# The dt projection moved into the first slot with its softplus steps issued without a break, the input squares moved later, and the SSD input projections of groups 1 to 7 in the two-instruction form

## The chip, the cores and the metric

The kernel runs on one core of a Trainium2 chip. The metric is device time in microseconds (us) of one launch; the profile also gives the span from the first to the last instruction of one profiled execution. Engines are named as in the profile: PE (matrix multiply) and PEld (its weight loads), DVE (vector), ACT (scalar, activations and copies), POOL and SP (which here only starts transfers). Each engine takes its instructions in the order in which they stand in its queue.

## The reference, cut to what matters

One layer with a sequence of 256 positions and width 2048: a Mamba-2 SSD mixer, a cross-attention and a gated FFN with a convolution, each as x + RMSNorm(f(RMSNorm(x))). The change touches the SSD mixer's input side:

```python
h = _rmsnorm(x, norm_pre[i, 0])
proj = h @ w_in                       # z 4096, x|B|C 6144, dt 64 columns
z, xbc, dt = jnp.split(proj, [SSD_D_INNER, SSD_D_INNER + SSD_CONV_DIM], axis=-1)
xbc = jax.nn.silu(_causal_dwconv(xbc, conv_w, conv_b))
dt = jax.nn.softplus(dt + dt_bias)
a = dt * (-jnp.exp(a_log))
a_cs = jnp.cumsum(a, axis=-1)
decay = jnp.exp(jnp.where(causal, a_cs[..., :, None] - a_cs[..., None, :], -jnp.inf))
y_diag = jnp.einsum('bgjcls,bcsgjp->bclgjp', cb[:, :, None] * decay, xdt)
```

Eight groups share B and C; each group has 8 of the 64 heads, that is four blocks of 128 columns of x and four of z.

## The kernel before

All matrices are fp32. To multiply them to fp32 accuracy on PE, each operand is split into a rounded part `hi` and a rest `lo` (`fp32r`), and three products are summed. A weight chunk of 128 columns by 2048 rows (1 MB) is loaded by SP into one of three `raw` buffers, and split in two halves of 8 row blocks: ACT copies `hi`, DVE subtracts `lo`. There are five buffers for `hi` halves and five for `lo` halves, so ACT may write a new half when PE has finished with the half five before it.

The input x lies transposed in `m` (16 row blocks of 128 by 256 positions). It is scaled by the norm's gain and split into `H[:, k]`, whose first 256 columns are `hi` and whose last 256 are `lo`. The norm's factor per position (`x_norm.rbc`, tile `rx`) comes later, since it commutes with the projection: `x_scaled` multiplies it in when a block's sum is taken out of PSUM. For the factor, ACT squares pairs of row blocks (`x_sq`), DVE adds the squares into `xacc`, eight tiny matmul records sum over partitions (`pe1`), POOL takes the power, and PE spreads it (`pe2`).

The projections run slot by slot. A slot has one or more lanes; a lane is one chunk, 16 row blocks k of three matmuls each (`mm3`: whi by x's hi, whi by x's lo, wlo by x's hi, 256 columns each), summed in one of four PSUM banks `pj`. The order of chunks is C0 and B0 together in slot 0, dt in a slot of its own, then x0, z0, x1, z1, x2, z2, x3, z3 of group 0, then C1, B1, x4, z4 and so on. The output projection's two halves stand after B4 and at the end. They, and the FFN, use `mm2`: whi by the 512 columns of x's hi and lo side by side, and wlo by x's hi in the upper half of the bank; the two halves of the bank are added when it is taken out. Work beside the matmuls is hooked to a slot and a place in it, and a scheduler with its own timeline decides each engine's final order from there, with `hot` for high priority.

The dt chunk has 64 columns, so its `hi` and `lo` are packed as one 128-column weight (`split_hi`, `split_lo` with kind "dt"), with two matmuls per k (`dt_mm`). `dt2` then turns its sum by a tiny matmul with `fold`, and computes the softplus in some 20 small DVE steps on 128 x 128 and one Exp on ACT; `dt3` sums along positions, `dt4` transposes the result and stores it to DRAM, from where `load_rows` reads it back spread over the partitions, and `decay`, `decay_exp` and `mk_m` make the masked decay matrices that `y_mm` needs.

Of the kernel before, what the change touches and what calls it, by code (L numbers as in the profile page):

```python
# [54 lines left out]

class Slot:
# [5 lines left out]
def hybrid_layer_kernel(ctx, tc, xT, memT, pvd, alog, w_dt, w_in, w_kv, w_q, w_out, w_o, w_up, w_dn, out):  # L62
    nc = tc.nc
    V, S, P, PE = nc.vector, nc.scalar, nc.gpsimd, nc.tensor
# [27 lines left out]
    B = {}  # L92
# [36 lines left out]
    def split_hi(c, h):  # L129
        kind = chunks[c][2]  # L130
        if kind == "dt":
            if h == 0:
                hi = splitp.tile([128, 1024], FR, name="hi")
                lo = splitp.tile([128, 1024], FR, name="lo")
                hi_t[c, 0], lo_t[c, 0] = hi, lo
                r = raw_t[c][:, :1024].rearrange("p (k n) -> p k n", n=64)
                for t, q in ((hi, 0), (lo, 8)):
                    S.activation(t.rearrange("p (k a n) -> p k a n", a=2, n=64)[:, :, 0], r[:, q:q + 8], AF.Copy)
            return
        a, b = span(c, h)  # L140
        hi_t[c, h] = g_part(c, h, 0) if c in in_g else splitp.tile([128, 1024], FR, name="hi")
        with behind(B.get("hold_s") if c in held else None):
            S.activation(hi_t[c, h][:, :b - a], raw_t[c][:, a:b], AF.Copy)  # L143

    def split_lo(c, h):
        kind = chunks[c][2]
        if kind == "dt":
            if h == 0:
                r = raw_t[c][:, :1024].rearrange("p (k n) -> p k n", n=64)
                for t, q in ((hi_t[c, 0], 0), (lo_t[c, 0], 8)):  # L150
                    t4 = t.rearrange("p (k a n) -> p k a n", a=2, n=64)
                    V.tensor_tensor(t4[:, :, 1], r[:, q:q + 8], t4[:, :, 0].bitcast(F32), op=OP.subtract)
            return
# [209 lines left out]
    def x_sq(j):  # L363
        sq = wA.tile([128, 2, T], F32, name="rows" if j else "xacc", bufs=4 if j else 1)
        S.activation(sq, pair(j), AF.Square)
        x_norm.add(sq)

    def x_scaled(ps, name="ev"):

        t = wA.tile([128, T], F32, name=name, bufs=2 if name == "ev" else 1)  # L370
        V.tensor_tensor(t, ps[:, :T], x_norm.rbc, op=OP.mult)  # L371
        return t

    def x_h(j):
        def fn():
            for k in range(2 * j, 2 * j + 2):
                now(hilo(halves(H[:, k]), m[:, k], col("pre", k)))
# [24 lines left out]
    def dt2():  # L402
# [22 lines left out]
        yield  # L425
# [3 lines left out]
        for t in range(2):  # L429
            V.scalar_tensor_tensor(a[:, t * NH:(t + 1) * NH], dtt[:, t], -1.0, nega, op0=OP.mult, op1=OP.mult)  # L430
# [194 lines left out]
    for kind, i in order:  # L625
        pos[kind, i] = 0 if kind == "B" and i == 0 else slot()
# [6 lines left out]
    for kind, i in order:  # L633
        s = pos[kind, i]
        if kind in ("C", "B"):
            blk = 32 + (8 if kind == "C" else 0) + i
            lane(s, w_in[blk_no], 2048, movH, bc_post(kind + "T", blk))
            blk_no += 1
            if kind == "B":
                hook(s + 2 if i else s + 3, "pe", cb_mm(i), 2 if i else 14)  # L640
        elif kind == "dt":
            c_dt = new_chunk(w_dt, 1024, "dt")
            slots[s].lanes.append((c_dt, 0, movH, hot(dt_post), dt_mm(c_dt), False))
            hook(s + 1, "pe", hot(dt2), 2)
            hook(s + 2, "pe", hot(dt3), 4)
            hook(s + 2, "pe", hot(dt4), 11)
        elif kind == "x":
            lane(s, w_in[blk_no], 2048, movH, xs_post(i))
            blk_no += 1
            d = 2 if i < 2 else 0  # L650
            if i == 0:
                for q in range(4):
                    hook(s + 2, "early", hot(load_rows(q)))
                    hook(s + 3, "early", decay(q))
                hook(s + 3, "early", decay_exp)
# [23 lines left out]
        elif kind == "z":  # L679
            lane(s, w_in[blk_no], 2048, movH, z_post(i))  # L680
# [391 lines left out]

    for j in range(KD // 2):
        if j % 2 == 0:
            hook(0, "pe", lambda j=j: w_first(j // 2), 4 * j)
        hook(0, "pe", x_h(j), 4 * j)
# [5 lines left out]
    for i, s in enumerate(slots):  # L1082
# [3 lines left out]
        if i == 0:  # L1086
            state["limit"] = 4
# [21 lines left out]
        names = ("pj", "pj", "pt", "py") if i == first_up else ("pj",) * 4  # L1109
# [138 lines left out]
```

## Time and profile before

| | |
|---|---|
| median of 3 runs | 1559.62 us (1558.85 to 1560.28) |
| the profiled execution's own time | 1559.15 us |
| its span | 1557.3 us |
| PE busy | 1541.5 us (99%) |
| DVE busy | 1199.2 us (77%) |
| ACT busy | 963.9 us (62%) |

The SSD input projections fill the stretch from 28.42 us to about 600 us, with the output projection's first half in between; group 1 is the stretch from 76.10 to 139.60 us, group 5 that from 418.10 to 480.60 us, and the FFN fills the stretch from 900 to 1400 us. PE is nearly always busy, so what counts is how many columns and instructions PE has to take, and where it has to wait for the others. A matmul's busy time in the profile overlaps the next one's; its pace is read from starts.

### The profile page before, as it was taken

What the parts mean: (1) busy time and instruction counts of PE and PEld (TensorE: products, weight loads), DVE (VectorE), ACT (ScalarE), POOL (GpSimd) and SP (SyncE); (2) the same over time, 40 slices, a digit from 0 to 9 for tenths busy, and PEclk for the clock granted to TensorE, in tenths of its full rate; (3) what the DMA queues carried; (4) which work ended last, traced back from release to release, by engine and by line L of the source; (5) the groups of instructions that cost most, each with busy time, mean ns of one, the idle gap of its engine ahead of it and who ended that gap; (6) DMA issues with size and microseconds to landing.
All of it is one profiled execution on the core that took longest, in us unless ns stands there. A gap on an engine that the chain in (4) does not pass through costs nothing. (4 is left out here: it accounts for less than half of the span.)

```text
span 1557.3 us, 26009 instructions
## 1 busy us (share of the span) xinstructions
PE 1541.5 (99%) x10364; PEld 1418.0 (91%) x10364; DVE 1199.2 (77%) x1903; ACT 963.9 (62%) x1566; POOL 11.3 (1%) x16
## 2 busy tenths in 40 slices
PE   9999999999999999999989999999999999999998
PEld 8999999989999999889888888888888888888886
DVE  7699989755898987969788878655787866778774
ACT  7698887644777774856566655544555533555553
POOL 0000000000000000000000000000000000000000
PEclk9999999999999999999999999999999999999999
DMA  7665555655455554854444555555555555555452
GB/s 278 212 217 189 174 203 190 194 191 184 162 204 177 167 186 136 324 189 165 161 153 146 194 190 189 192 183 199 190 191 191 184 187 198 194 192 189 151 212 78
DMA packets 50937, 292.10 MB, mean 188 GB/s; under 512 B 5568, under 2 KB 9728, under 8 KB 23936
## 3 DMA queue, kind: packets, MB, share of 16 engines
q1 hardware_dynamic: 50096, 289.34, 54.3%
q8 instruction: 81, 1.33, 0.3%
q10 hardware_dynamic: 720, 1.11, 0.2%
q14 instruction: 40, 0.33, 0.1%
HBM read 288.26 MB, written 2.16 MB: 186 GB/s over the span
## 5 line engine op out<-in xcount | busy, mean ns | idle before, releaser
L143 ACT ACTIVATE hi<-raw 128x1024 fp32r<-128x1024 f32 (+2 forms) x518 | 539.9, 1045 | 480.9 <-PE pj L252 378.4
L157 DVE TENSOR_TENSOR lo<-raw,hi 128x1024 fp32r<-128x1024 f32 (+2 forms) x518 | 624.4, 1207 | 252.7 <-ACT hi L143 247.9
L252 PE MATMUL pj<-H,hi 128*128 128x512 f32 x1344 | 466.6, 392 | 1.1 <-DVE ev L931 1.1
L252 PE MATMUL pj<-G,hi 128*128 128x512 f32 x1202 | 417.1, 392 | 0.0
L246 PE MATMUL pj<-H,hi 128*128 128x256 f32 x1344 | 379.1, 283 | 1.3 <-ACT hi L266 0.8
L248 PE MATMUL pj<-H,lo 128*128 128x256 f32 x1344 | 377.9, 282 | 0.8 <-DVE lo L268 0.7
L247 PE MATMUL pj<-H,hi 128*128 128x256 f32 x1344 | 377.8, 281 | 0.0
L253 PE MATMUL pj<-H,lo 128*128 128x256 f32 x1344 | 376.2, 280 | 0.0
L253 PE MATMUL pj<-G,lo 128*128 128x256 f32 x1202 | 335.8, 280 | 0.0
L252 PEld LDWEIGHTS pj<-H,hi 128*128 128x128 f32 x1344 | 252.3, 188 | 57.0 <-ACT hi L143 1.3
L252 PEld LDWEIGHTS pj<-G,hi 128*128 128x128 f32 x1202 | 225.4, 188 | 49.5
L246 PEld LDWEIGHTS pj<-H,hi 128*128 128x128 f32 x1344 | 253.3, 189 | 3.2 <-ACT hi L266 1.6
L248 PEld LDWEIGHTS pj<-H,lo 128*128 128x128 f32 x1344 | 253.3, 189 | 2.1 <-DVE lo L268 1.7
L247 PEld LDWEIGHTS pj<-H,hi 128*128 128x128 f32 x1344 | 253.7, 189 | 1.2 <-DVE H L272 0.2
L253 PEld LDWEIGHTS pj<-H,lo 128*128 128x128 f32 x1344 | 252.5, 188 | 0.1
L253 PEld LDWEIGHTS pj<-G,lo 128*128 128x128 f32 x1202 | 225.8, 188 | 0.4
L941 DVE SCALAR_TENSOR_TENSOR fu<-ev,pv,fu 128x255 f32<-128x255 f32 (+1 forms) x176 | 84.3, 480 | 2.8
L460 DVE SCALAR_TENSOR_TENSOR u<-ev,pv,u 128x255 f32<-128x255 f32 (+2 forms) x144 | 68.7, 479 | 5.1 <-ACT u L456 3.9
L937 ACT ACTIVATE fu<-ev,pv 128x256 f32<-128x256 f32 x88 | 51.7, 589 | 1.4 <-DVE ev L934 0.9
L371 DVE TENSOR_TENSOR ev<-pj,rx 128x256 f32<-128x256 f32 x80 | 33.7, 422 | 13.4 <-PE pj L248 10.7
L266 ACT ACTIVATE Mh<-dec 128x768 fp32r<-128x768 f32 x32 | 26.9, 841 | 16.4 <-PE py L248 15.6
L934 DVE TENSOR_TENSOR ev<-ev,rb 128x256 f32<-128x256 f32 x84 | 35.5, 422 | 1.4
(287 smaller groups left out, 1461.7 us busy)
## 6 DMA issues: line engine op xcount, KB each, us to landing
raw<-in_w_up_dram SPq DMA_DIRECT2D x88, 1024.0 KB, 4.8
raw<-in_w_in_dram SPq DMA_DIRECT2D x78, 1024.0 KB, 4.9
raw<-in_w_out_dram SPq DMA_DIRECT2D x32, 1024.0 KB, 4.8
raw<-in_w_dn_dram SPq DMA_DIRECT2D x32, 960.0 KB, 4.7
raw<-in_w_dn_dram SPq DMA_DIRECT2D x16, 896.0 KB, 4.4
rows<-rows_d SPq DMA_DIRECT2D x32, 256.0 KB, 4.4
raw<-in_w_kv_dram SPq DMA_DIRECT2D x4, 1024.0 KB, 4.8
raw<-in_w_kv_dram SPq DMA_DIRECT2D x8, 512.0 KB, 4.3
```

Of the source, the lines that this page charges most:

```text
L143: S.activation(hi_t[c, h][:, :b - a], raw_t[c][:, a:b], AF.Copy)
L157: V.tensor_tensor(lo_t[c, h][:, :b - a], raw_t[c][:, a:b], hi_t[c, h][:, :b - a].bitcast(F32), op=OP.subtract)
L246: PE.matmul(ps, whi, xhi, start=start, stop=False)
L247: PE.matmul(ps, whi, xlo, start=False, stop=False)
L248: B["mm"] = PE.matmul(ps, wlo, xhi, start=False, stop=stop)
L252: PE.matmul(ps, whi, x, start=start, stop=False)
L253: B["mm"] = PE.matmul(ps[:, T:], wlo, x[:, 0:T], start=False, stop=stop)
L371: V.tensor_tensor(t, ps[:, :T], x_norm.rbc, op=OP.mult)
L460: V.scalar_tensor_tensor(u[:, d:], ps[:, :T - d], pv[:, w + j:w + j + 1], u[:, d:], op0=OP.mult, op1=OP.add)
L934: V.tensor_tensor(t, t, B["n4"].rbc, op=OP.mult)
L937: S.activation(u, t, AF.Identity, bias=col("fb", blk), scale=pv[:, w + 2:w + 3])
L941: V.scalar_tensor_tensor(u[:, d:], t[:, :T - d], pv[:, w + j:w + j + 1], u[:, d:], op0=OP.mult, op1=OP.add)
```

## The change

Slot 0 now holds three lanes: C0, B0 and dt. dt's weights come in two transfers among those of C0 and B0, into the tile `dec` which is free at that time, and are split by `dt_split` at two places of the slot; its matmuls follow those of C0 and B0 by four row blocks, in the bank `pt`. The chunk of x0 is loaded right behind the input, since the third `raw` buffer is free now. All later slots have numbers lower by one.

The squares of the input wait for the last of the splits into `H` (`behind(B["x_hi"])`), so ACT does them after the first slot's splits.

The softplus is cut into `dt2` and `dt2b`, hooked to the slots of x0, z0 and x1. While it runs, `B["chain"]` holds its last step, and `Behind` puts every DVE instruction that is issued meanwhile behind that step. The decay steps of group 0 move from the start to the end of their slot.

B, C, x and z of groups 1 to 7 (70 chunks) use `mm2` in place of `mm3`. Their `x_scaled` has two steps more: ACT copies the bank's upper half to SBUF, and DVE adds the lower half before it multiplies.

```diff
+class Behind:
+    def __init__(self, tc, engine, book):
+        self.tc, self.engine, self.book = tc, engine, book
+    def __getattr__(self, name):
+        fn = getattr(self.engine, name)
+        def f(*args, **kw):
+            x = self.book.get("chain")
+            with self.tc.issue_after(x.ins) if x is not None else nullcontext():
+                return fn(*args, **kw)
+        return f
...
-    V, S, P, PE = nc.vector, nc.scalar, nc.gpsimd, nc.tensor
+    B = {}
+    V, S, P, PE = Behind(tc, nc.vector, B), nc.scalar, nc.gpsimd, nc.tensor
...
     def x_sq(j):
         sq = wA.tile([128, 2, T], F32, name="rows" if j else "xacc", bufs=4 if j else 1)
-        S.activation(sq, pair(j), AF.Square)
+        with behind(B["x_hi"]):
+            S.activation(sq, pair(j), AF.Square)
...
-    def x_scaled(ps, name="ev"):
+    def x_scaled(ps, name="ev", wide=False):
         t = wA.tile([128, T], F32, name=name, bufs=2 if name == "ev" else 1)
-        V.tensor_tensor(t, ps[:, :T], x_norm.rbc, op=OP.mult)
+        if wide:
+            S.activation(t, ps[:, T:], AF.Copy)
+            V.tensor_tensor(t, ps[:, :T], t, op=OP.add)
+            V.tensor_tensor(t, t, x_norm.rbc, op=OP.mult)
+        else:
+            V.tensor_tensor(t, ps[:, :T], x_norm.rbc, op=OP.mult)
...
-        def fn(ps, k):
-            w = (hi_t if k < 8 else lo_t)[c, 0][:, (k % 8) * 128:(k % 8 + 1) * 128]
...
+        def fn(ps, i):
+            for k in range(max(0, i - 4), i - 3 if i < KD - 1 else KD):
...
+    def dt2b():
+        x, a, e, z, z2, p = B["dtw"]
         V.tensor_scalar(a, e, 2.0, None, op0=OP.add)
         V.reciprocal(p, a)
-        yield
         V.tensor_tensor(z, e, p, op=OP.mult)
         V.tensor_tensor(z2, z, z, op=OP.mult)
+        B["chain"] = V.tensor_scalar(p, z2, 2.0 / 15, None, op0=OP.mult)
         yield
-        V.tensor_scalar(p, z2, 2.0 / 15, None, op0=OP.mult)
         for i in (13, 11, 9, 7, 5, 3):
-            V.scalar_tensor_tensor(p, p, 2.0 / i, z2, op0=OP.add, op1=OP.mult)
+            B["chain"] = V.scalar_tensor_tensor(p, p, 2.0 / i, z2, op0=OP.add, op1=OP.mult)
...
-        pos[kind, i] = 0 if kind == "B" and i == 0 else slot()
+        pos[kind, i] = 0 if (kind, i) in (("B", 0), ("dt", 0)) else slot()
...
-            lane(s, w_in[blk_no], 2048, movH, bc_post(kind + "T", blk))
+            lane(s, w_in[blk_no], 2048, movH, bc_post(kind + "T", blk), wide=i > 0)
...
-            hook(s + 1, "pe", hot(dt2), 2)
-            hook(s + 2, "pe", hot(dt3), 4)
-            hook(s + 2, "pe", hot(dt4), 11)
+            hook(s + 1, "pe", hot(dt2), 8)
+            hook(s + 2, "pe", hot(dt2b), 6)
+            hook(s + 3, "pe", hot(dt3), 4)
+            hook(s + 3, "pe", hot(dt4), 10)
+            hook(s + 5, "early", lambda: B.pop("chain"))
...
-            lane(s, w_in[blk_no], 2048, movH, xs_post(i))
+            lane(s, w_in[blk_no], 2048, movH, xs_post(i), wide=i >= 4)
...
-            lane(s, w_in[blk_no], 2048, movH, z_post(i))
+            lane(s, w_in[blk_no], 2048, movH, z_post(i), wide=i >= 4)
...
+        if j in (0, 2):
+            nc.sync.dma_start(raw_t[2][:, 256 * j:256 * j + 512], chunks[2][0][:, 256 * j:256 * j + 512])
+    issue_dma(3)
```

The scheduler's result on DVE before, at the place where the softplus stands: its steps are the rows with `cbm_428`; `lo_498` and `lo_584` are halves of weight chunks, `u` and `ev` belong to convolutions.

```order
L412 SCALAR_TENSOR_TENSOR cbm_428<-cbm_428 128x128
L460 SCALAR_TENSOR_TENSOR u_348<-ev_349,pv_69,u_348 128x253
L460 SCALAR_TENSOR_TENSOR u_360<-ev_361,pv_69,u_360 128x253
L157 TENSOR_TENSOR lo_498<-raw_341,hi_496 128x1024
L415 TENSOR_SCALAR cbm_428<-cbm_428 128x128
L371 TENSOR_TENSOR ev_502<-pj_418,rx_319 128x256
L157 TENSOR_TENSOR lo_584<-raw_341,hi_582 128x1024
L416 RECIPROCAL cbm_428<-cbm_428 128x128
L268 TENSOR_TENSOR CT_356<-xsT_347,CT_356 128x256
```

On DVE after the change, at the same place (line L68 is the wrapper's): the softplus steps are those with `cbm_447`, and `lo_573` is the second half of z1's weights.

```order
L68 SCALAR_TENSOR_TENSOR u_487<-ev_488,pv_69,u_487 128x253
L68 TENSOR_SCALAR cbm_447<-cbm_447 128x128
L68 RECIPROCAL cbm_447<-cbm_447 128x128
L68 TENSOR_TENSOR cbm_447<-cbm_447 128x128 x2
L68 TENSOR_SCALAR cbm_447<-cbm_447 128x128
L68 SCALAR_TENSOR_TENSOR cbm_447<-cbm_447 128x128 x7
L68 SCALAR_TENSOR_TENSOR dtt_88<-cbm_447 128x128
L68 SCALAR_TENSOR_TENSOR cbm_447<-dtt_88,nega_91 128x64 x2
L68 TENSOR_TENSOR cbm_560<-ms_553,tri_75 128x2x128
L68 TENSOR_TENSOR lo_573<-raw_375,hi_571 128x1024
```

Before, splits and evictions stood between the steps; after, they follow in one run and `lo_573` stands behind it.

On ACT after the change, the queue ahead of the softplus' Exp (line L420), from the split `hi_654` (second half of x2) to the second table load behind it; `hi_660` is the first half of z2.

```order
L149 ACTIVATE hi_654<-raw_385 128x1024
L472 ACT_TABLE_LOAD
L472 ACTIVATE xsT_391<-u_392 128x256
L472 ACTIVATE xsT_403<-u_404 128x256
L264 ACTIVATE CT_400<-xsT_391 128x256
L466 ACTIVATE u_487<-ev_488,pv_69 128x256
L416 ACTIVATE cbm_447<-ms_444 128x128
L264 ACTIVATE BT_412<-xsT_403 128x256
L149 ACTIVATE hi_660<-raw_480 128x1024
L420 ACT_TABLE_LOAD
L420 ACTIVATE cbm_447<-cbm_447 128x128
L472 ACT_TABLE_LOAD
```

Before, this Exp stood ahead of the first Silu with one table load behind it; now it stands behind a Silu and `hi_660`, with a table load on either side.

On PE after the change, around the middle of z1 (bank `pj_685`): `hi_571` and `lo_573` are its second half, `pj_784` is x2's bank, `ms_598` is the sum along positions.

```order
L246 MATMUL pj_685<-H_70,lo_484 128x256
L244 MATMUL pj_685<-H_70,hi_571 128x256
L245 MATMUL pj_685<-H_70,hi_571 128x256
L244 MATMUL pj_784<-H_70,hi_577 128x256
L245 MATMUL pj_784<-H_70,hi_577 128x256
L548 MATMUL pt_604<-ident_74,xsT_486 128x128 x2
L446 MATMUL ms_598<-cbm_447,tri_75 128x64 x2
L447 MATMUL ms_598<-cbm_447,after_76 128x64
L246 MATMUL pj_685<-H_70,lo_573 128x256
```

The rows of the softplus' result now stand between the two halves of z1, which before they didn't; there they stood two slots later.

## Rows read from the trace of the kernel before

**Rows 1.** The page, part 1: busy us, share of the span, instructions.

```profile
PE 1541.5 (99%) x10364; PEld 1418.0 (91%) x10364; DVE 1199.2 (77%) x1903; ACT 963.9 (62%) x1566; POOL 11.3 (1%) x16
```

**Rows 2.** Stretches: length, busy PE, PEld, DVE, ACT, POOL (instructions), clock, DMA share, GB/s.

```profile
900.00:1400.00 500.00, 500.00 (x2887) 439.93 (x2886) 358.55 (x533) 261.07 (x383) 0.00 (x0) 1.00 0.56 190
76.10:139.60 63.50, 63.50 (x527) 62.85 (x525) 59.44 (x97) 57.37 (x98) 0.00 (x0) 1.00 0.60 205
418.10:480.60 62.50, 62.50 (x520) 61.98 (x519) 54.10 (x88) 46.59 (x81) 0.00 (x0) 1.00 0.55 186
```

**Rows 3.** PE's timeline: slot 0, norm, first matmuls of x0, z0, z1, x2.

```profile
6.66 0.56 PE L246 MATMUL pj<-H,hi 128*128 128x256 f32 x1
...
23.55 0.95 PE L304 MATMUL ms<-ones,xacc 128*128 128x1 f32 x8
24.36 0.36 PE L393 MATMUL pj<-H,hi 128*128 128x256 f32 x1
...
28.42 0.28 PE L246 MATMUL pj<-H,hi 128*128 128x256 f32 x1
...
34.49 0.28 PE L246 MATMUL pj<-H,hi 128*128 128x256 f32 x1
...
45.76 0.28 PE L246 MATMUL pj<-H,hi 128*128 128x256 f32 x1
...
51.61 0.28 PE L246 MATMUL pj<-H,hi 128*128 128x256 f32 x1
```

**Rows 4.** ACT's timeline: first slot, then the split of x0's weights.

```profile
8.68 1.71 ACT L270 ACTIVATE H<-m,pv 128x256 fp32r<-128x256 f32 x4 [1.98 <-DMA m<-in_xT_dram]
10.30 1.14 ACT L365 ACTIVATE rows<-m 128x512 f32<-128x512 f32 x2
11.34 1.13 ACT L266 ACTIVATE hi<-raw 128x512 fp32r<-128x512 f32 x2
...
25.28 2.01 ACT L143 ACTIVATE hi<-raw 128x1024 fp32r<-128x1024 f32 x2 [2.94 <-DMA raw<-in_w_in_dram]
```

**Rows 5.** Busy time of the stretch from 12 to 16 us.

```profile
12.00:16.00 4.00, 3.91 (x26) 3.33 (x26) 4.00 (x9) 4.00 (x9) 0.00 (x0) 1.00 1.04 412
```

**Rows 6.** DVE's timeline: two weight splits, the norm's factor.

```profile
26.37 2.36 DVE L157 TENSOR_TENSOR lo<-raw,hi 128x1024 fp32r<-128x1024 f32 x2 [1.68 <-ACT hi L143]
28.65 0.42 DVE L332 COPY rx<-ms 128x256 f32<-128x256 f32 x1
```

**Rows 7.** ACT's timeline: a table load, a Silu, a split that waits for PE.

```profile
37.05 1.28 ACT L462 ACT_TABLE_LOAD   x1
38.35 0.42 ACT L462 ACTIVATE xsT<-u 128x256 f32<-128x256 f32 x1
...
45.84 1.06 ACT L143 ACTIVATE hi<-raw 128x1024 fp32r<-128x1024 f32 x1 [1.65 <-PE pj L247]
```

**Rows 8.** DVE's timeline: steps of the softplus.

```profile
40.89 0.95 DVE L416 RECIPROCAL cbm<-cbm 128x128 f32<-128x128 f32 x1
...
53.93 0.28 DVE L424 SCALAR_TENSOR_TENSOR cbm<-cbm 128x128 f32<-128x128 f32 x1
54.24 0.29 DVE L427 SCALAR_TENSOR_TENSOR dtt<-cbm 128x128 f32<-128x128 f32 x1
```

**Rows 9.** PE's timeline at a wait near 804 us; two stretches (columns of rows 2).

```profile
801.66 0.43 PE L324 MATMUL ms<-ident,nr 128*128 128x128 f32 x2 [1.08 <-POOL nr L315]
804.78 0.79 PE L246 MATMUL pj<-H,G 128*128 128x256 f32 x2 [2.69 <-ACT H L53]
...
802.00:804.70 2.70, 0.10 (x1) 0.00 (x0) 2.63 (x6) 0.48 (x1) 0.00 (x0) 0.68 0.51 127
804.70:809.70 5.00, 4.43 (x19) 4.14 (x20) 4.97 (x11) 3.29 (x7) 0.00 (x0) 0.50 0.34 143
```

**Rows 10.** Instruction groups of group 5: count, busy us, mean ns, idle before, releaser.

```profile
L371 DVE TENSOR_TENSOR ev<-pj,rx 128x256 f32<-128x256 f32 x10 | 4.2, 421 | 2.4 <-PE pj L248 2.3
...
L143 ACT ACTIVATE hi<-raw 128x1024 fp32r<-128x1024 f32 x21 | 22.1, 1055 | 12.3 <-PE pj L247 12.2
```

More of the change, by code (lines that the diff above doesn't have):

```diff
@@ L376, in fn @@
             for k in range(2 * j, 2 * j + 2):
-                now(hilo(halves(H[:, k]), m[:, k], col("pre", k)))
+                hi, lo = halves(H[:, k])
+                B["x_hi"] = S.activation(hi, m[:, k], AF.Copy, scale=col("pre", k))
+                V.scalar_tensor_tensor(lo, m[:, k], col("pre", k), hi.bitcast(F32), op0=OP.mult, op1=OP.subtract)
         return fn
@@ L390, in dt_mm @@
     def dt_mm(c):
-        def fn(ps, k):
-            w = (hi_t if k < 8 else lo_t)[c, 0][:, (k % 8) * 128:(k % 8 + 1) * 128]
-            PE.matmul(ps[:, :T], w, H[:, k, 0:T], start=(k == 0), stop=False)
-            PE.matmul(ps[:, :T], w, H[:, k, T:], start=False, stop=(k == KD - 1))
+        def fn(ps, i):
+            for k in range(max(0, i - 4), i - 3 if i < KD - 1 else KD):
+                w = (hi_t if k < 8 else lo_t)[c, 0][:, (k % 8) * 128:(k % 8 + 1) * 128]
+                PE.matmul(ps[:, :T], w, H[:, k, 0:T], start=(k == 0), stop=False)
+                PE.matmul(ps[:, :T], w, H[:, k, T:], start=False, stop=(k == KD - 1))
         return fn
@@ L450, in hybrid_layer_kernel, with conv @@
     ssd_norm = Norm(wA, DI, keep=ry)
-    def conv(ps, blk, dst):
+    def conv(ps, blk, dst, wide):
         u = wA.tile([128, T], F32, name="u", bufs=3)
-        ps = x_scaled(ps)
+        ps = x_scaled(ps, wide=wide)
         w = PV["cw"] + 4 * blk
@@ L466, in post @@
             t = wA.tile([128, T], F32, name="xsT", bufs=2)
-            yield from conv(ps, blk, t)
+            yield from conv(ps, blk, t, blk % 8 > 0)
             yield
@@ L528, in post @@
             t = wA.tile([128, T], F32, name="xsT", bufs=2)
-            yield from conv(ps, i, t)
+            yield from conv(ps, i, t, i >= 4)
             B["xsT", i] = t
@@ L566, in post @@
             t = wA.tile([128, T], F32, name="sz", bufs=2)
-            S.activation(t, x_scaled(ps), AF.Silu)
+            S.activation(t, x_scaled(ps, wide=i >= 4), AF.Silu)
             B["sz", i] = t
@@ L652, in hybrid_layer_kernel @@
                 for q in range(4):
-                    hook(s + 2, "early", hot(load_rows(q)))
-                    hook(s + 3, "early", decay(q))
-                hook(s + 3, "early", decay_exp)
+                    hook(s + 3, "early", hot(load_rows(q)))
+                    hook(s + 3, "late", decay(q))
+                hook(s + 3, "late", decay_exp)
             elif i % 4 == 0:
@@ L1041, in hybrid_layer_kernel @@
     hook(first_up + 1, "pe", lambda: [run(p, ps) for p, ps in B["late"]][:0], 0)
-    for c in (0, 1, 2):
+    for c in (0, 1):
         raw_t[c] = rawp.tile([128, 2048], F32, name="raw")
+    raw_t[2] = dec.rearrange("p a n -> p (a n)")
     for h in range(2):
@@ L1071, in w_first, with dt_split @@
             now(hilo((hi_t[c, j // 2][:, q], lo_t[c, j // 2][:, q]), raw_t[c][:, 512 * j:512 * (j + 1)]))
+    def dt_split(j):
+        if j == 0:
+            hi_t[2, 0] = splitp.tile([128, 1024], FR, name="hi")
+            lo_t[2, 0] = splitp.tile([128, 1024], FR, name="lo")
+        t = (hi_t, lo_t)[j][2, 0].rearrange("p (k a n) -> p k a n", a=2, n=64)
+        now(hilo((t[:, :, 0], t[:, :, 1]), raw_t[2][:, 512 * j:512 * j + 512].rearrange("p (k n) -> p k n", n=64)))
     for j in range(KD // 2):
         if j % 2 == 0:
[L1075 to L1076 removed]
+            hook(0, "pe", lambda j=j: w_first(j // 2), 6 * j)
+        hook(0, "pe", x_h(j), 6 * j)
+        if j in (1, 5):
+            hook(0, "pe", lambda j=j: dt_split(j // 4), 6 * j)
         hook(0, "tail", lambda j=j: x_sq(j))
```

35 lines of the change are left out of this document (8 added, 27 removed).

## The prediction

> **What bounds the kernel now.** Read first the busy shares: PE is busy for 99% of the span [rows 1]. Then the stretches: in group 1, in group 5 and in the FFN PE is busy for all of the time at full clock (1.00), while DVE is busy for 59.4 of 63.5 us in group 1, 54.1 of 62.5 in group 5 [rows 2]. So from the start of x0 on, the time of the SSD stage is PE's own stream. The groups of group 5 show what paces the weight splits: ACT stood idle for 12.2 us before them because PE had not yet freed a buffer [rows 10]. They run ahead of PE and cover most waits. Last, the timelines of the first 55 us: there PE does wait. It starts at 6.66 and reaches x0 at 28.42 [rows 3], while it had 128 matmuls of 256 columns for slot 0 and dt.
>
> **The wide form.** From z0's first matmul at 34.49 to z1's at 45.76 stand 96 matmuls [rows 3]: 117.4 ns each, so a row block of three costs 352.2 ns. In the FFN 2887 matmuls in 500 us [rows 2] are 1443.5 pairs: 346.4 ns a row block of the two-instruction form. The gain is 5.8 ns for each of 70 x 16 = 1120 row blocks: 6.5 us. Lower bound 4 us, if the 512-column form is a little slower beside the SSD work than in the FFN; upper bound 9.5, if the 1 us that group 1 takes longer than group 5 [rows 2] goes away too in groups 1 to 3.
> The Trainium skill speaks against that size: its page "TensorE: Matmul & The Clock Gate", section "Back-to-back issue gap", has columns / 2.4 GHz plus 2.5 ns per matmul, by which one instruction less saves 2.5 ns. By it the term would be 2.8 us. The trace has 117.4 ns where the rule has 109.2, so the rows decide, and the case is kept as a rival.
> The price of the form is an ACT copy and a DVE add per block, at most 0.42 us on DVE (the mean of a 256-column eviction [rows 10]). For ten blocks that is 4.2 us per group. In group 5 DVE has 62.5 - 54.1 = 8.4 us idle and takes it at no cost. In group 1 it has 4.1 us [rows 2], just what is added. I cost it at nothing, because the splits run ahead; without that cover it is a rival below.
>
> **The start.** ACT bounds the first slot, not the DMA: from 8.68 on 14 scalings of 0.405 (x4 from 8.68 to 10.30), 6 splits and 2 dt splits of 0.52 (x2 from 11.34, like the squares from 10.30) [rows 4] make 9.8 us, so it ends at 18.7, small waits included. Of the 4.7 MB of x, C0, B0 and dt, 3.4 are still to land at 8.68, 8.3 us at 412 GB/s [rows 5], so until 17.0. The squares stand behind: five (2.6 us) ahead of x0's first split, whose 1 MB has landed by then (17.0 and 2.5 us). That split takes 0.96 us and its `lo` 1.14 (half of 2.36 less the overlap, with its end 1.2) [rows 6]: x0 starts in earnest at 23.75, 4.7 us earlier than now. DMA order and SP's queue cost nothing here, since ACT is later than both.
> x0 ends at 29.15. z0 now holds the norm's matmuls (0.81 us, 23.55 to 24.36 [rows 3]) and its transposes (0.4) and ends at 36.05. x1 needs C0's bank: the norm's factor, placed late in z0 by the queue's order, comes at 35.1; factor 0.5, `yt` 0.34 and `ev` 0.42 end at 36.4, so x1 starts at 36.45 and ends (5.64 and 0.4 for `fold`) at 42.5, 3.3 us ahead of now (45.76).
>
> **The hold in z1.** Now follow the queues. The split `hi_654` may start when PE has done half of x1, at 39.3, and ends at 40.3; a table load of 1.28 [rows 7] follows, two Silus, two copies and `u` until 43.75 (0.31 to 0.5 each). `hi_660` waits for x1's end, as the split at 45.84 does now [rows 7], and takes until 44.7. Then come another load to 46.1 and Exp to 46.4. DVE's run starts at 46.5: a step 0.26, the reciprocal 0.93, then eleven steps that each wait for the last, 0.31 each (53.93 to 54.24 [rows 8]), and two that don't, 5.0 us in all; `cbm` 0.35 and `lo_573` 1.2 end at 53.0. Before, `lo` halves and evictions filled the gaps between these steps, and no split waited for them.
> PE has for z1, from 42.5, 24 matmuls (2.8), six for `ms_553` (0.66) and four that stand ahead (0.47); from 46.45 it waits, but for 0.55 us of transposes and sums, until 53.05. It then needs 22 more for z1: 55.65. At this point it has done 1.35 us of work (sums, `ms_553`, two matmuls of x2) that before came later; before it stood there at 51.61 [rows 3]. So the start costs 55.65 - 51.61 - 1.35 = 2.7 us, say 2.5. Bounds: -3.3 if nothing holds `lo_573` (x1's lead is kept), +5 if two or three of the waits are a microsecond longer.
> **The clock.** PE waited near 802 us too: hardly anything between 801.66's transposes and 804.78, and 0.50 of the clock (1.2 GHz) from there to 809.70, in 5 us of work [rows 9]. A wait of 6.6 us with 0.55 of work in it should lower it as well. If it stays low for 4.6 us after, half of that work is lost: 2.2 us. Bounds 0 and 5.
> The rest (`decay` later in its slot, `load_rows`, dt's buffer, one ACT activation at the start) lies beside PE: the first `y_mm` moves by a block at most, and splits are ahead again by then. From the output projection's second half on, the queues stand as before.
>
> **The sum,** against the profiled execution's 1559.15: - 6.5 + 2.5 + 2.2 = - 1.8, so 1557.35. The median of the runs is 0.47 above that execution: 1557.8 us.
>
> **Rivals.**
> No hold: Exp or the run comes earlier than the queues let me think, and `lo_573` is in time; then the start gains 3.3 and the clock stays: 1559.6 - 6.5 - 3.3 = 1549.8. For it: before, the steps cost PE nothing. Against: the three queues above, each in fixed order.
> The hold without the clock: PE's scattered work or a shorter wait keeps 2.4 GHz. 1559.6 - 6.5 + 2.5 = 1555.6.
> The clock falls twice: PE also waits 2.3 us ahead of x0. Another 2.2: 1560.0. For it, the fall near 803 came with a wait of 2.7 us [rows 9]; against, an earlier one of 1.1 us was just ahead of it.
> Less gain: the 512-column instruction costs 3.3 ns more here than in the FFN, so that 2.5 of the 5.8 ns are left, 2.8 us. Then 1559.6 - 2.8 + 4.7 = 1561.5. Against it is the FFN's row over 500 us; no row of the SSD groups has this form yet. This is the case that the page named above stands for.
> Slower, by DVE in groups 1 to 3: with 4.2 us added to 4.1 us idle, evictions fall behind until one of the four banks is not free. This decides once DVE's idle time in a group is used up. Price: the 1 us per group by which these are longer already is not regained, the gain of these groups (3 x 0.93 = 2.8) is lost, and one wait for a bank per group costs about 1.7 (split 0.96, eviction 0.76): 1557.8 + 2.8 + 5.1 = 1565.7. Against it: DVE's busy time in group 1 includes y work left over from group 0, for the same group takes 54.1 later.
>
> **Numbers.** Hold and low clock, as summed: 0.46, its own range 1555 to 1560.5. No hold 0.15, hold without the clock 0.13, clock twice 0.08, less gain 0.05, slower 0.13. From no hold's 1549.8 to where DVE's rival begins, 1564.5, is held 8 times in 10. A measurement can tell about 0.2%, 3.1 us, from no change: faster is below 1556.5. That takes no hold, the hold without the clock and three tenths of the first case: 0.42. Slower than 1562.7 is DVE's rival and a little of the clock's and the small gain's: 0.15. The rest, 0.43, is the same.
>
> **What would show it.** In the profile of the changed kernel: 1120 matmul records fewer, and in groups 1 to 7 row blocks of 346 to 348 ns at full clock; x0's first `lo` matmul near 23.7; on ACT `hi_660`, a load and Exp ending near 46.4; on DVE a run of dependent steps for 5 us and then `lo`; on PE a wait of about 6 us in the middle of z1, put down to DVE, and 0.50 of the clock behind it. The prediction is wrong if PE has no wait of 3 us there, if the clock stays at 1.00 up to 60 us, if row blocks of the new form cost 350 ns or more, or if PE waits in groups 1 to 3.

## The result and the profile after

The changed kernel takes 1567.43 us (median of 4 runs, 1566.55 to 1568.41) against 1559.23 us beside it (1558.21 to 1560.28): ratio 1.0052, 95% interval 1.004 to 1.0065. It is slower by 8.2 us, where 1.8 us less were forecast. The first part of the page, which answers to [rows 1]:

```profile
PE 1539.1 (98%) x9244; PEld 1366.9 (87%) x9244; DVE 1220.2 (78%) x1973; ACT 985.3 (63%) x1639; POOL 12.2 (1%) x16
```

PE has the 1120 records fewer that were to go, and DVE and ACT have some 70 more each. The view of PE's waits from 14 to 745 us (idle us, times, longest) shows what is new; in the kernel before PE waited nowhere between 22 and 744 us:

```profile
PE ms L446 <- DVE cbm L68: 3.0, 1, 3.0
PE pj L250 <- DVE ev L68: 2.6, 1, 2.6
PE pj L250 <- ACT hi L149: 1.9, 1, 1.9
PE pt L548 <- ACT xsT L472: 1.7, 1, 1.7
PE pj L250 <- DVE G L68: 1.2, 1, 1.2
PE pj L250 <- DVE m L68: 0.8, 1, 0.8
PE pj L244 <- DVE ev L68: 0.6, 1, 0.6
PE pj L246 <- DVE lo L68: 0.6, 1, 0.6
```

Rows 1 and 4 are the hold in z1 that was forecast, the last two stand ahead of x0 and x1. The other four were not forecast: 6.5 us in front of blocks of the wide form or of the output projections. PE's timeline places them (x0's first `lo` product, x1, the two parts of the hold, z1 going on, the first blocks of group 1, the fourth and fifth block of it, its eighth, the first of group 2, the two halves of the output projection, and the instruction at 804.78 in [rows 9]):

```profile
24.16 0.39 PE L246 MATMUL pj<-H,lo 128*128 128x256 f32 x1 [0.56 <-DVE lo L68]
37.15 0.36 PE L244 MATMUL pj<-H,hi 128*128 128x256 f32 x1 [0.57 <-DVE ev L68]
...
49.23 0.44 PE L548 MATMUL pt<-ident,xsT 128*128 128x128 f32 x2 [1.70 <-ACT xsT L472]
52.63 1.09 PE L446 MATMUL ms<-cbm,tri 128*128 128x64 f32 x4 [2.96 <-DVE cbm L68]
...
54.14 0.58 PE L246 MATMUL pj<-H,lo 128*128 128x256 f32 x1
...
80.88 0.39 PE L250 MATMUL pj<-H,hi 128*128 128x512 f32 x1
...
99.05 0.40 PE L250 MATMUL pj<-H,hi 128*128 128x512 f32 x1
...
105.44 0.39 PE L250 MATMUL pj<-H,hi 128*128 128x512 f32 x1
...
127.25 0.49 PE L250 MATMUL pj<-H,hi 128*128 128x512 f32 x1 [2.63 <-DVE ev L68]
...
146.74 0.40 PE L250 MATMUL pj<-H,hi 128*128 128x512 f32 x1
...
309.24 0.50 PE L250 MATMUL pj<-G,hi 128*128 128x512 f32 x1 [0.81 <-DVE m L68]
...
658.26 0.49 PE L250 MATMUL pj<-G,hi 128*128 128x512 f32 x1 [1.89 <-ACT hi L149]
...
813.40 0.58 PE L244 MATMUL pj<-H,G 128*128 128x256 f32 x1 [2.69 <-ACT H L53]
```

Stretches of the same run, columns as in [rows 2]: group 1, group 5, then three in which the granted clock is 0.50:

```profile
80.88:146.74 65.86, 63.23 (x361) 55.32 (x359) 60.04 (x99) 57.83 (x103) 0.00 (x0) 0.97 0.56 194
422.85:484.37 61.52, 61.52 (x363) 54.19 (x361) 54.56 (x95) 48.45 (x89) 0.00 (x0) 1.00 0.54 191
...
49.97:56.80 6.83, 4.17 (x18) 4.02 (x19) 6.58 (x15) 1.18 (x4) 0.00 (x0) 0.50 0.24 67
128.48:131.89 3.41, 3.41 (x12) 2.87 (x11) 3.41 (x8) 2.79 (x7) 0.00 (x0) 0.50 0.57 156
753.12:756.53 3.41, 3.41 (x18) 3.41 (x18) 2.32 (x5) 0.97 (x1) 0.00 (x0) 0.50 0.76 293
```

The balance is taken up to the same instruction, 804.78 [rows 9] against 813.40: the changed kernel is 8.6 us later there. Of these, 4.8 are there when group 1 begins (76.10 [rows 2] against 80.88). The four new waits stretch the distance from one start to the next by 2.8 (127 us), 1.0 (309), 1.3 (632) and 2.0 us (658), 7.1 together. The last two low clocks cost half of 3.41 us each, 3.4. These make 15.3; what lies between that and 8.6 is the gain of the wide form, **6.7 us**. In group 5, where nothing waits, it is 62.50 [rows 2] less 61.52, 0.98 us for 160 row blocks, 6.1 ns each.

Only two of the four new waits are waits for a bank: those at 127 and 309 us end when DVE has taken a sum out (`ev`, `m`). The one at 632 us ends when DVE has made the projection's operand `G`, the one at 658 us when ACT has split a half of weights (`hi`).

How the bank comes late in group 1 is seen in the timelines. The eighth block, at 127.25, takes the bank of the fourth, which PE filled from 99.05 to 105.44. DVE takes sums out of the banks in their order; the fourth is the last row:

```profile
101.41 0.43 DVE L68 TENSOR_TENSOR ev<-pj,ev 128x256 f32<-128x256 f32 x1
...
111.56 0.42 DVE L68 TENSOR_TENSOR ev<-pj,ev 128x256 f32<-128x256 f32 x1
...
126.77 0.42 DVE L68 TENSOR_TENSOR ev<-pj,ev 128x256 f32<-128x256 f32 x1 [0.38 <-ACT ev L371]
```

It ends at 127.19, 21.7 us after PE left the bank. In that time PE has the three other banks to fill, at 5.5 to 6.9 us a block: it was through with them 19.0 us after 105.44, and waited for the rest. ACT's timeline shows what stood ahead of its part of that eviction, the copy:

```profile
119.23 1.28 ACT L522 ACT_TABLE_LOAD   x1
120.52 2.77 ACT L522 ACTIVATE dec<-dec 128x3072 f32<-128x3072 f32 x1
...
124.75 1.28 ACT L472 ACT_TABLE_LOAD   x1
126.05 0.42 ACT L472 ACTIVATE xsT<-u 128x256 f32<-128x256 f32 x1
126.37 0.37 ACT L371 ACTIVATE ev<-pj 128x256 f32<-128x256 f32 x1
```

### The profile page after: what moved, and what is told of

Same layout as the page of the kernel before. It is cut to its first block, busy times and chain, and to the rows that moved or that the text cites. A ratio compares the mean times of both kernels' runs of the same rounds, so it can differ in the third digit from the quotient of the medians.

```text
span 1566.0 us, 23943 instructions
## 1 busy us (share of the span) xinstructions
PE 1539.1 (98%) x9244; PEld 1366.9 (87%) x9244; DVE 1220.2 (78%) x1973; ACT 985.3 (63%) x1639; POOL 12.2 (1%) x16
## 5 line engine op out<-in xcount | busy, mean ns | idle before, releaser
L250 PE MATMUL pj<-H,hi 128*128 128x512 f32 x2464 | 863.0, 393 | 3.7 <-DVE ev L68 2.6
L250 PEld LDWEIGHTS pj<-H,hi 128*128 128x128 f32 x2464 | 463.5, 188 | 103.3 <-DVE ev L68 2.9
L155 DVE TENSOR_TENSOR lo<-raw,hi 128x1024 fp32r<-128x1024 f32 (+2 forms) x264 | 314.7, 1193 | 168.3 <-ACT hi L149 165.6
L68 DVE TENSOR_TENSOR lo<-raw,hi 128x1024 fp32r<-128x1024 f32 (+1 forms) x262 | 314.1, 1206 | 73.5 <-ACT hi L149 71.0
L68 DVE SCALAR_TENSOR_TENSOR u<-ev,pv,u 128x255 f32<-128x255 f32 (+2 forms) x144 | 68.4, 479 | 8.9 <-ACT u L466 7.7
L244 PE MATMUL pj<-H,hi 128*128 128x256 f32 x224 | 63.7, 286 | 1.4 <-ACT hi L264 0.9
L245 PE MATMUL pj<-H,hi 128*128 128x256 f32 x224 | 63.3, 284 | 0.0
L244 PEld LDWEIGHTS pj<-H,hi 128*128 128x128 f32 x224 | 42.6, 191 | 2.2 <-ACT hi L264 1.3
L245 PEld LDWEIGHTS pj<-H,hi 128*128 128x128 f32 x224 | 42.8, 191 | 0.2 <-DVE H L68 0.2
L68 DVE SCALAR_TENSOR_TENSOR yt<-xsT,pv,py 64x256 f32<-64x256 f32 x64 | 30.6, 478 | 7.2 <-PE py L246 6.6
```

Source lines behind the costliest of these rows:

```text
L68: return fn(*args, **kw)
L244: PE.matmul(ps, whi, xhi, start=start, stop=False)
L245: PE.matmul(ps, whi, xlo, start=False, stop=False)
L250: PE.matmul(ps, whi, x, start=start, stop=False)
```

## The experiments

Two theories to begin with: the wide form's longer eviction (an ACT copy and one more DVE instruction) is too much where DVE and ACT are both full; or the new start makes these queues late. Each run is compared with the kernel before on the same chip; its median there was 1559.2 to 1560.3 us.

**The wide form alone (e1_wide_only).** The kernel before, with the part of the diff that hands `wide` through `lane`, `conv`, `z_post` and `x_scaled`.

> The kernel before with the wide form of groups 1 to 7 and nothing else of the change. Theory (the eviction of a wide block goes through ScalarE's and VectorE's queues, which run up to 22 us behind in group 1 and late at the two output projections, so banks come free too late): the old start stays, the row blocks gain about 6.7 us, and PE waits remain of 0.9 to 2.1 us near the first and second output projection (together some 4 us) and perhaps one of 0 to 3 us with a clock fall in group 1: 1556 to 1561 us. Rival (the late start is what made the queues late, the wide form costs nothing by itself): no PE wait over 0.5 us between 60 and 740 us, 1552.5 us.

Measured 1564.5 us (1563.7 to 1564.81), ratio 1.0031 (1.0019 to 1.0043), more than either theory said. The waits of PE from 76 to 745 us:

```profile
PE pj L252 <- DVE ev L373: 5.5, 1, 5.5
PE pj L252 <- ACT hi L143: 1.4, 1, 1.4
PE pj L252 <- DVE G L272: 1.2, 1, 1.2
PE pj L252 <- DVE m L617: 0.4, 1, 0.4
```

The same four places, with the start untouched, and the wait in group 1 is twice as long. So the late start is not what makes the banks late; with it the wait in group 1 is even 2.9 us shorter. That is most of why the parts (5.2 us here, 6.5 below) do not add up to 8.2. That the queues work off their load while PE stands in z1 would explain it, but was not tried by itself. What ended the 5.5 us is seen in two rows, ACT's Exp of the decays and DVE's eviction:

```profile
114.67 2.76 ACT L517 ACTIVATE dec<-dec 128x3072 f32<-128x3072 f32 x1
...
119.47 0.42 DVE L373 TENSOR_TENSOR ev<-pj,ev 128x256 f32<-128x256 f32 x1 [2.97 <-ACT ev L372]
```

DVE stood idle for 2.97 us ahead of that eviction: it waited for the copy, which stood behind the Exp and its two table loads (5.3 us together) in ACT's queue.

**The first-slot change alone (e2_start_only).** The changed kernel with `wide=False` throughout.

> The changed kernel with all input projections of the state-space part back in the narrow form: the first-slot change alone. Theory (start and wide form add): the wait of some 5 us in the z1 block and the clock fall stay, nothing else waits until 740 us, 1559.2 + 4.8 = 1564.0 us. Rival (the late decays of the new start are what blocks group 1): the wait of about 2.8 us near 127 us and its clock fall are there in the narrow form too, 1567 to 1569 us.

Measured 1565.78 us (1564.48 to 1566.16), ratio 1.0039 (1.0027 to 1.0052). That is 1.8 more than the theory's 1564.0 and less than the rival's 1567: in this profile group 1 begins at 81.60, 5.5 us later than before, where it was 4.8 in the changed kernel. PE's waits from 45 to 140 us are the hold and one of 0.2 us at 126.5:

```profile
PE ms L446 <- DVE cbm L68: 3.0, 1, 3.0
PE pt L548 <- ACT xsT L472: 2.0, 2, 1.8
```

**Group 1 narrow again (e3_wide_from_g2).** In the changed kernel `i >= 4` becomes `i >= 8`, and B and C are wide from group 2 on.

> The changed kernel with group 1 in the narrow form, groups 2 to 7 wide. Theory (only group 1 has ScalarE and VectorE both full): the wait at 127 us (2.8 us) and the clock at 0.50 behind it (1.7 us) are gone, a seventh of the gain (0.95 us) is given up: 1567.4 - 4.5 + 0.95 = 1563.9 us. Rival (the backlog is in every group and the wait moves to group 2): a bank wait of 2 us or more between 146 and 215 us, 1567 to 1569 us.

Measured 1564.42 us (1563.19 to 1564.93), ratio 1.0031 (1.0019 to 1.0042): 3.0 less than the changed kernel, 3.5 expected. The wait for a bank near 127 us is gone (0.4 us for a transpose is left there), and none came in group 2.

**Which of the two queues?** First the right half copied by DVE (e4_copy_dve):

```diff
-            S.activation(t, ps[:, T:], AF.Copy)
+            V.tensor_copy(t, ps[:, T:])
```

> The changed kernel with the right half of a wide block copied out by VectorE in place of ScalarE, for the state-space blocks alone. Theory (ScalarE's in-order queue, with the decays, Exp and two table loads ahead of the copy, is what holds the bank at 127 us): that wait shrinks under 1 us, the waits at the output projections stay or grow, about 1563 to 1565 us. Rival (VectorE's work is the limit, it gets 0.42 us more in each block): the wait in group 1 grows over 4 us and others appear in groups 2 to 4, 1569 us or more.

Measured 1581.31 us (1580.45 to 1585.9), ratio 1.0147 (1.0132 to 1.0162). With ACT out of the eviction none of the four banks comes late in group 1, but the group took 71.21 us instead of 65.86: PE waited there 4.7 us for other things that DVE and ACT make (2.0, 1.3, 0.9 and 0.5 us, ahead of `y_mm` and of the product of C and B). The theory's 1563 to 1565 us fell. Since DVE had one instruction more in each block, this does not clear ACT's queue. The other way round, the multiplication went to POOL, on the start of before (e6_wide_pool):

```diff
-            V.tensor_tensor(t, t, x_norm.rbc, op=OP.mult)
+            P.tensor_tensor(t, t, x_norm.rbc, op=OP.mult)
```

> The kernel before with groups 1 to 7 wide as in the wide-alone run (1564.5 us), but the multiplication by the norm factor of a wide block on GpSimd, so that VectorE has one instruction for each block, as before the change. Theory (VectorE's added 0.34 to 0.42 us for each block is what makes the banks late): the 5.6 us wait in group 1 falls under 1 us and the waits at the projections under 0.5 us each: 1553 to 1556 us. Rival (the copy's place in ScalarE's queue makes them late): the wait in group 1 stays over 3 us, 1560 us or more. A GpSimd instruction of this size does not occur in the trace; if it slows VectorE or comes late itself, the time lies above the theory's too, and VectorE's mean durations in group 1 show it.

Measured 1568.74 us (1567.55 to 1571.22), ratio 1.0058 (1.0045 to 1.007). In group 1 (64.43 us against 69.95 of the wide form alone) it helped, the wait fell from 5.5 to 2.5 us. But POOL takes 1331 ns there for what DVE does in 420, and new waits of 0.4 to 1.6 us came in the later groups. So it did not tell the two apart. The stretch of group 1, and in it POOL's group (busy, mean ns, idle before):

```profile
75.97:140.40 64.43, 61.88 (x361) 54.25 (x360) 59.10 (x91) 56.41 (x98) 10.64 (x8) 1.00 0.55 198
```

```profile
L374 POOL TENSOR_TENSOR ev<-ev,rx 128x256 f32<-128x256 f32 x8 | 10.6, 1331 | 102.0 <-DVE ev L373 102.0
```

The clean form leaves the multiplication out (e10_no_mult), so that the norm factor is missing in wide blocks:

> The wide form alone in groups 1 to 7 (1564.5 us), with the multiplication by the norm factor of a wide block left out, which leaves that factor out of the result: ScalarE's copy stays, VectorE has one instruction of 0.42 us for each block, as before the change. Theory (VectorE's added work is the cause): the wait of 5.6 us in group 1 falls under 0.6 us, the waits at the output projections under 0.6 us each, 1560.0 - 6.7 = 1553.3 us, with up to 1.5 us more for waits that stay. Rival (ScalarE's copy in its late queue holds the banks): the wait in group 1 stays over 3 us, 1560 us or more.

Measured 1554.92 us (1554.16 to 1556.02), ratio 0.9973 (0.9963 to 0.9982). ACT's copies are all there; DVE has one instruction a block, as before. The waits at the projections are gone, one of 1.1 us is left in group 1, and at the instruction at 744.11 us of the kernel before PE is 6.6 us ahead (737.51), which is about the forecast gain. So without DVE's added 0.42 us a block the form pays. That ACT's queue has no part in the long wait is not shown: the 1.1 us stand behind the same Exp, and the scheduler, with less on DVE, put one more block's eviction ahead of that Exp. A copy moved ahead of the Exp with both DVE instructions kept, or more than the two `ev` buffers that a copy writes to, was not tried. Group 1 with and without the multiplication, first of e1_wide_only, then of e10_no_mult:

```profile
76.27:146.22 69.95, 64.46 (x367) 56.53 (x366) 62.13 (x104) 59.73 (x108) 0.00 (x0) 0.95 0.54 186
```

```profile
75.34:138.35 63.01, 61.89 (x362) 54.23 (x361) 58.01 (x93) 58.10 (x104) 0.00 (x0) 1.00 0.59 202
```

**The form only where DVE has time.** Groups 2 to 6 were meant, on the old start; but the first kernel (e5_wide_g2_6) had the bounds `0 < i < 7`, so groups 1 to 6 were wide:

> The kernel before, its start untouched, with the wide form in groups 2 to 6 alone; groups 1 and 7 stay narrow. Theory (a wide block costs only where VectorE has no idle time left: group 1, and the end of group 7, where the second output projection waits for the last gated blocks): no PE wait over 0.5 us before 740 us, five sevenths of the 6.7 us: 1559.3 - 4.8 = 1554.5 us. Rival (the longer eviction costs in every group): waits between 140 and 600 us, 1558 us or more.

Measured 1563.04 us (1562.46 to 1563.93), ratio 1.0021 (1.0012 to 1.003). Read for what it was, it tells something else: with group 7 narrow both waits ahead of the second projection are gone, and group 1 still waits 5.5 us. With the bounds as meant (e9_wide_g2_to_6):

> The kernel before, its start untouched, with the wide form in groups 2 to 6 and groups 1 and 7 narrow (in the run named e5_wide_g2_6 group 1 was still wide). Theory (VectorE has no idle time in group 1 and is late for the second output projection in group 7; elsewhere its added work is covered): no PE wait over 0.6 us before 740 us, five sevenths of the 6.7 us: 1560.0 - 4.8 = 1555.2 us. Rival (the longer eviction costs in every group, the group that comes first pays): a wait of 2 us or more in groups 2 to 4, 1558 us or more.

Measured **1554.52 us** (1553.61 to 1555.41), ratio 0.9969 (0.9958 to 0.9981), faster than both kernels. PE has no wait between 76 and 735 us. Group 1 (narrow) and group 3 (wide):

```profile
76.51:140.02 63.51, 63.51 (x526) 62.86 (x525) 59.61 (x97) 57.61 (x98) 0.00 (x0) 1.00 0.59 205
202.52:264.12 61.60, 61.60 (x362) 54.27 (x361) 57.38 (x102) 51.29 (x95) 0.00 (x0) 1.00 0.54 191
```

**What the start costs.** Without the uninterrupted run (e7_start_no_chain):

```diff
-    V, S, P, PE = Behind(tc, nc.vector, B), nc.scalar, nc.gpsimd, nc.tensor
+    V, S, P, PE = nc.vector, nc.scalar, nc.gpsimd, nc.tensor
```

> The first-slot change alone (1565.8 us), without the uninterrupted run of the time-step instructions: VectorE may again take other work between them. Theory (the run of some 5 us holds back the low part of the z1 weights and costs the PE wait of 5 us and the clock fall): both are gone, 1565.8 - 6 = 1560 us or less. Rival (the steps' results are what PE waits for, and they come later when they are mixed): PE waits as long, at the cumulative sums, or later at the first outputs, 1565 us or more.

Measured 1570.06 us (1569.56 to 1570.34), ratio 1.0063 (1.005 to 1.0075): the theory fell. z1 has no wait and group 1 begins at 74.25, 1.8 us ahead of the kernel before. But the softplus ends at 59.99, where the changed kernel had 52.23, the first decay starts at 76.5, and PE stands in group 1 instead, with a low clock behind it (waits from 45 to 140 us):

```profile
PE pj L244 <- DVE ev L375: 3.5, 1, 3.5
PE pt L548 <- ACT xsT L472: 2.1, 2, 1.1
PE py L244 <- DVE yt L590: 1.7, 1, 1.7
```

With the hold kept, but filled (e8_start_fill):

```diff
+            for _ in range(26 if i == 0 else 0):
+                with tc.issue_after(x.ins):
+                    PE.matmul(ps[:, T:], H[:, 0, 0:128], H[:, 0, 0:T], start=True, stop=True)
```

> The first-slot change alone (1565.8 us) with 26 added matmuls of 256 columns, whose output nothing reads, in the middle of the z1 wait: they take 26 x 0.117 = 3.0 us of the 3.1 us in which PE stood idle. Theory (the clock at 0.50 for 6.8 us is the answer to the idle time): the clock stays at 1.00, and the matmuls behind the wait run at 117 ns in place of 214: about 2 us less, 1563.8 us. Rival (it falls anyway, or the waits are the whole cost): 1565.5 to 1566 us.

Measured 1566.25 us (1565.29 to 1567.4), ratio 1.0037 (1.0024 to 1.0051). The clock did stay at 1.00 (49.30 to 56.80 us), and group 1 began 1.6 us earlier than in e2_start_only (80.03 against 81.60). But the decays began at 76.1 us (why so late is not shown), and two waits for banks in group 1, 2.4 us, took it back. Then earlier decays with the hold as it is (e11_start_acs_act):

```diff
-        V.tensor_copy(acs.rearrange("p a b -> p (a b)"), ps[:, :2 * NH])
+        S.activation(acs.rearrange("p a b -> p (a b)"), ps[:, :2 * NH], AF.Copy)
```

> The first-slot change alone (1565.8 us), with the copy of the cumulative sums out of PSUM done by ScalarE, which is idle there, in place of VectorE, where it stands behind six splits and ends 7 us after its matmul. Theory (what the new start costs is that the decays begin at 70.9 to 71.7 us in place of 66.8, so that group 1, where VectorE is full, ends as much later): the first decay starts at 66 us or earlier, group 1 ends at 140 to 142 us in place of 145.6, 1560.5 to 1562 us. Rival (the wait of 5 us in z1 and the clock fall are the cost, the decays have room): 1565 us or more.

Measured 1567.33 us (1564.64 to 1567.85), ratio 1.005 (1.0037 to 1.0062). The decays start at 63.9 us, and nothing is won: group 1 had no wait for a bank to lose, and PE had one wait of 0.5 us more behind z1's hold and the clock at 0.50 for 10.2 us. The hold and its clock, the rival, are what PE loses here. Both together, filling and early decays (e14_fill_acs_act):

> The first-slot change alone with the 26 filling matmuls in z1's wait and the copy of the cumulative sums on ScalarE. With the copy alone it was 1567.3 us (the clock at 0.50 for 10.2 us, no wait in group 1), with the filling alone 1566.3 us (the clock at 1.00, but decays at 76.1 us and 2.7 us of waits in group 1). Theory (the filling takes away the clock's cost of 2 to 4 us, and early decays let group 1 keep it): 1563 to 1565 us. Rival (group 1 gives any earlier start back): waits of over 2 us between 100 and 130 us, 1566 us or more.

Measured 1563.67 us (1562.61 to 1565.96), ratio 1.0024 (1.0015 to 1.0033): as the theory had it. Against e8_start_fill, which differs in the copy alone, it is 2.6 us less: the decays begin at 63.5 us instead of 76.1, and the two waits for banks in group 1 are gone. So late decays do cost, once the clock is kept up. Two rows of its busy time, from the hold and from group 1, with the clock at 1.00 in both:

```profile
49.30:56.80 7.50, 6.99 (x57) 6.81 (x58) 7.16 (x18) 2.72 (x7) 0.00 (x0) 1.00 0.21 50
80.00:100.00 20.00, 20.00 (x164) 19.68 (x164) 19.46 (x30) 19.28 (x41) 0.00 (x0) 1.00 0.60 207
```

No hold and the copy on ACT (e13_no_chain_acs_act):

> The first-slot change alone without the uninterrupted run of the time steps (1570.1 us: no wait in z1, but 8.2 us of waits between 100 and 130 us), with the copy of the cumulative sums on ScalarE. Theory (with z1's wait gone the bound passes to the decays, which began at 76.5 us there): they begin some 5 us earlier, the waits of group 1 shrink by as much, 1564 to 1566 us. Rival (group 1 waits for VectorE's amount of work, whenever the decays begin): the 8 us stay, 1569 us or more.

Measured 1570.66 us (1570.01 to 1571.22), ratio 1.0069 (1.0056 to 1.0082), but it decides nothing: without the run the copy is not what is late (the softplus itself ends at 60.2), the decays began at 77.2 us, and the waits stayed much as they were. Last, the wide form in groups 2 to 6 on two of these starts. On that of e11_start_acs_act (e12_both_acs_act):

> The changed kernel with the copy of the cumulative sums on ScalarE and the wide form in groups 2 to 6 alone. Theory (the two causes, late decays and a full VectorE in group 1, add): the time of the run with ScalarE's copy alone less 4.8 us, 1556 to 1557 us. Rival (the new start costs through z1's wait, and the wide form in every group): 1561 us or more.

Measured 1560.29 us (1559.45 to 1561.62), ratio 1.0008 (0.9999 to 1.0016). On that of e13_no_chain_acs_act:

> The run named e13_no_chain_acs_act with the wide form in groups 2 to 6 alone. Theory (the wide form in these groups gives 4.7 us whatever the start is, as it did on the start of before and, from 1567.3 to 1560.3 us, on the new start): 4.7 us less than that run, 1559 to 1561 us. Rival (a late group 1 makes the wide groups behind it late): less than 3 us less.

Measured 1564.42 us (1562.22 to 1565.16), ratio 1.0025 (1.0014 to 1.0036). That is 7.0 and 6.2 us less than the same starts in the narrow form, against 4.7 on the start of before. That the form gives more on these starts is not shown: in the first pair, the profile of the narrow form had the low clock for 3.41 us longer behind the hold and once more, for 3.41 us, at 753 us, together worth 3.4 us. Groups 2 to 6 have no wait behind a late group 1.

## Why the prediction was wrong

**The wide form's gain** was forecast at 6.5 us, 5.8 ns a row block; the balance gives 6.7, and group 5 gives 6.1 ns. By the gap that the Trainium skill gives for an isolated matmul ("TensorE: Matmul & The Clock Gate", "Back-to-back issue gap") it would be an estimated 2.8 us, 0.4 in group 5; the trace has 0.98 there, so the rows decide against it.

**Its extra eviction is the step that failed.** The prediction put it: "I cost it at nothing, because the splits run ahead". The splits' lead was the wrong cover to look at. In group 1 PE needs a free bank, and that depends on how long after a block's last matmul the block is taken out: 21.7 us, where the three other banks lasted for 19.0. The cost is 7.1 us of waits and, behind the first, a low clock of 1.7 us. Of the 7.1 us 3.8 are waits for a bank; 1.3 at 632 us are for the operand `G` and 2.0 at 658 us for a half of weights, so that "from the output projection's second half on, the queues stand as before" did not hold either. Between the forecast of 1.8 us less and the profile's 8.6 us more lie 10.4 us: 8.8 are this step, 1.7 the fall of the clock at 753 us, for which the sum had no term, and the other terms are off by 0.1 and 0.2. Of the signs of being wrong that the prediction names, "PE waits in groups 1 to 3" came, in group 1.

e1_wide_only shows the cost with the old start, e10_no_mult shows that nearly all of the waiting goes when DVE's added instruction goes, and e3_wide_from_g2 and e5_wide_g2_6 show that the places go when group 1 and group 7 are narrow. How much of the wait in group 1 is DVE's load and how much the copy's place in ACT's queue stays open. The rival "slower, by DVE in groups 1 to 3" named DVE and was near in size (1565.7) but was given 0.13. That the size is near is partly luck: it counted a wait in each of groups 1 to 3, but groups 2 and 3 wait nowhere, and the output projections were not in it.

**The start** came in the order that was worked out, each date 0.4 to 1.1 us later. x0's first `lo` product: 24.16 (forecast 23.75); x1: 37.15 (36.45). The end of Exp and the start of DVE's run:

```profile
47.14 0.31 ACT L420 ACTIVATE cbm<-cbm 128x128 f32<-128x128 f32 x1
```

```profile
47.49 0.23 DVE L68 TENSOR_SCALAR cbm<-cbm 128x128 f32<-128x128 f32 x1 [1.10 <-ACT cbm L420]
...
52.87 1.22 DVE L68 TENSOR_TENSOR lo<-raw,hi 128x1024 fp32r<-128x1024 f32 x1
```

Exp ends at 47.45 (46.4), the run begins at 47.49 (46.5), the `lo` half is there at 54.09 (53.0), and PE goes on with z1 at 54.14 (53.05). It waited 1.7 and 3.0 us with transposes between them, not six in one piece, and for the steps themselves first, since the sums stand ahead of the `lo` products in its queue.

**The clock** was at 0.50 (1.2 GHz) for 6.83 us from 49.97 on, after PE's wait of 1.7 us, and the start cost 4.8 us up to group 1 where 2.5 + 2.2 = 4.7 were forecast. That the sum is so near is partly luck. The same start put group 1 at 80.73 to 81.88 us in four profiles, and the old one at 75.34 to 77.53 in six. And e8_start_fill, where the clock stayed up, began group 1 1.6 us earlier than e2_start_only. An estimate from that is 1.6 us for the clock and 3.2 for the hold: one term was forecast too high, the other too low. That the low clock has a price of its own is also shown by e14_fill_acs_act against e11_start_acs_act: 3.7 us by the medians, on two chips, and 3.3 us by where group 1 begins (79.71 against 83.05), for a clock that was low for 10.2 us.

**"The rest nothing"** held in the changed kernel, for a reason that the prediction did not see. The decays begin at 70.9 us, 4.1 later than before, but the hold makes PE late as well. Where the hold is gone (e7_start_no_chain) the decays begin later still, PE waits for evictions in group 1, and the kernel is slower; e8_start_fill against e14_fill_acs_act shows that late decays bring such waits. Part of their lateness is the transfers: DVE's splits stand behind the run in its queue, so that DVE splits no weights from 33.4 to 52.9 us. No `raw` buffer comes free, 1 GB/s moves from 42 to 54 us, and then four weight chunks go out between 54 and 64 us, in front of the small ones (two stretches of the changed kernel, DMA share and GB/s last):

```profile
42.00:54.00 12.00, 7.34 (x55) 6.88 (x54) 8.40 (x23) 8.34 (x14) 0.00 (x0) 0.83 0.01 1
55.50:64.00 8.50, 8.50 (x69) 8.50 (x68) 8.40 (x15) 4.44 (x10) 0.00 (x0) 0.92 0.95 360
```

The transfers of the sums (`rows`) go out at 65.2 us instead of 63.5 before, and the first takes 5.7 us instead of 3.3. That this crowding is what delays them was not tried by itself. Also open: a start with neither hold nor late decays; e13_no_chain_acs_act was meant to be one and was not.

## What to carry to other kernels

An instruction added to every eviction is paid for stage by stage: compare the time from a block's last matmul to its bank's release with the time of as many blocks as there are other banks (three here), and not the engine's busy share or the lead of its other work. Look for what stands ahead of each part of the eviction in its engine's queue, such as an Exp between two table loads. Use the cheaper form only in the stages that have room, as the version with groups 2 to 6 does (1554.5 us). And when a wait is taken away at one place, look for the next engine's date behind it before counting the gain: without the run (e7_start_no_chain) or with the hold filled (e8_start_fill), PE waited in group 1 instead.

## What the runs showed of the hardware that was not expected

The clock fell to 0.50 for 3.41 us at 753 us in the changed kernel, after PE waits of 0.3 and 0.4 us. The kernel before has the same two waits at 744 and 745 us, and the clock stays at 1.00; of the 17 profiles 9 have this fall, with the same instructions around it. At 1.7 us a fall it may be part of why runs of one kernel do not agree to the microsecond; each kernel has one profile, so this is not shown.

POOL's two-input instruction on 128 x 256 took 1331 ns in group 1 of e6_wide_pool, 3.2 times DVE's 420. The Trainium skill ("GPSIMD Engine Reference", "3.1 Elementwise — side-by-side cycle accounting") has 1.96 times, for an add over 2048 columns; at this size the measurement is worse than that.
